# Output projection of a hybrid encoder block by one level of Strassen's scheme

## The chip, the cores and the metric

The kernel runs on one core of a Trainium2 chip. The metric is the device time of one execution in microseconds (us), of which the median of several runs is compared. Below, "the projection" is the product of the gated sum m with W_o, and "the MLP's first layer" is what follows it.

## What is computed

The kernel computes one block of an encoder on 1024 tokens of width 1024 (MLP width 4096). The part that the change touches is the line with `w_o`:

```python
merged = jax.nn.sigmoid(ga) * y_a + jax.nn.sigmoid(gb) * y_b
x = x + merged @ w_o[l]
h = rms_norm(x, norm2_g[l]) @ w_mlp_in[l]
x = x + jnp.square(jax.nn.relu(h)) @ w_mlp_out[l]
```

All operands are float32. A matmul of the kernel works on float16, so each operand is scaled by a power of two and split in a high half (float16 of the value, made by ACT) and a low half (float16 of the remainder, made by DVE), and each product is run in three passes (high by high, high by low, low by high, `PASSES`). A product of 1024x1024 by 1024x512 in plain form is thus 8 token blocks x 8 channel blocks x 3 passes = 192 matmuls of 128x512.

## The kernel before, in words

**Order of the work.** After attention and the convolution, eight gate stages n = 0 to 7 run, one for each 128 channels of m. A stage computes both gates of its channels by a Strassen level already (`seven`, L1273: 7 products of 12 matmuls, 18.1 us) and the two branch products (`branch_units`, L1331: 48 matmuls). Stages 0 to 6 do the gates first. Stage 7 does the branches first (503.97 to 514.33 us in the trace) and its gates last (514.33 to 532.48), with a sigmoid and a product for each half of the tokens (`post7`, `post3`, `last`). Each m_n is split by `m_done` (`last` for n = 7) into mH and mL, [128, 8 channel blocks, 1024 tokens].

**The projection** (532.48 to 615.60) comes next: columns 0 to 511 of W_o are the chunk cO[0], columns 512 to 1023 are cO[1]. A call of `proj(b, half)` (L1605) is a unit of 24 matmuls of 128x512 for token block b, and its result is added to the residual X1 by one DVE instruction (L1610). There are 16 such units. Their weights are split by `Chunk.prep` (L280: ACT L343, DVE L330), with a maximum of each row (L362) and a sum over all partitions by a small matmul (`all_sum`, L226) behind one cast (L372), from which the scale follows.

**The MLP's first layer** then takes two strips of 256 columns in two halves each (`quad`, 615.60 to 633.90 and 633.90 to 652.30: 14 units of 12 matmuls of 128x256) and 14 strips of 512. It needs the normalised rows of X1 in Strassen forms: blocks b and b+4 are a pair, and for each pair n the ACT squares the rows (`square`, L1430), DVE and ACT make the factor (`row_scale`, L1436), ACT applies it (`normal`, L1442), DVE makes four sums and differences (`form_sums`, L1480), ACT the highs and DVE the lows (`high`, `low`, L1468 and L1472). `first1`/`prep1(0)` makes the first strips' weights beside it (lines L1234, L1238; sums on POOL, L1221). The second layer follows to the end.

**What sets the order.** Each engine runs its own queue strictly in the order in which the program emits the instructions. `unit` (L233) emits a unit's matmuls, then the posts (the instructions that read the results) of the unit before, then it advances generators: `step` those of the list `fg`, `tick` those of the list `bg`, one piece at a time. A generator yields at `yield`, and `yield WAIT` gives the turn back. So where a piece of preparation stands in an engine's queue depends on how many units, steps and ticks came ahead of it. PSUM results rotate through eight banks named ps_d, ps_s and ps_o; a unit can start only when the post of the unit that last used its bank is done. Weights come by DMA into five raw buffers; a new load starts when `done` counts a finished one (`load_upto`).

## Time and profile before

| | |
|---|---|
| median of 3 runs (lowest to highest) | 1201.63 us (1200.84 to 1201.65) |
| profiled execution, its own time | 1201.78 us |
| span from the first to the last instruction | 1200.0 us |
| granted TensorE clock | 1.00 |
| gate products of stage 7 | 514.33 to 532.48 |
| projection | 532.48 to 615.60 (384 matmuls of 128x512) |
| first two half strips of the MLP | 615.60 to 633.90, 633.90 to 652.30 |

The execution's own time and its span differ by 1.8 us, which lie outside the instructions. PE is TensorE with its matmuls, PEld its weight loads, DVE, ACT and POOL are the vector, scalar and GpSimd engines. The profile gives the busy time of each; `a <-b` behind a row's idle time says that the engine stood idle before it and that b ended that. The table of windows gives a stretch's length, then the busy time (and number of instructions) of PE, PEld, DVE, ACT and POOL in it, then the granted clock, the DMA share and GB/s.

### The profile page before, as it was taken

How to read it: one execution, taken by the hardware profiler on the slowest of the kernel's cores; microseconds unless marked ns; L12 is line 12 of the kernel's file. 1: busy time of each engine (PE TensorE's matmuls, PEld its weight loads, DVE VectorE, ACT ScalarE, POOL GpSimd, SP SyncE). 2: the span in 40 equal slices, each digit the busy share in tenths (PEclk: the TensorE clock that was granted, in tenths of full speed). 3: DMA queues.
4: the chain of work that ended last, by engine and by line, in shares of the span. 5: the costliest groups of instructions: out<-in, count | busy, mean ns of one | idle time of the engine just before them, and what ended most of it. 6: DMA issues, size and time to landing. Idle time of an engine off the chain costs nothing.

```text
span 1200.0 us, 16982 instructions
## 1 busy us (share of the span) xinstructions
PE 1190.2 (99%) x6272; PEld 574.7 (48%) x6272; DVE 940.3 (78%) x1750; ACT 752.1 (63%) x1181; POOL 450.9 (38%) x296
## 2 busy tenths in 40 slices
...
GB/s 259 201 153 126 107 96 145 124 163 117 135 121 58 54 70 36 71 116 165 60 170 195 174 142 192 160 130 193 153 242 220 356 73 193 158 120 214 105 36 105
DMA packets 162707, 171.25 MB, mean 143 GB/s; under 512 B 123328, under 2 KB 123840, under 8 KB 158528
## 3 DMA queue, kind: packets, MB, share of 16 engines
...
## 4 chain that ended last, share of the span: by engine, by line
PE 84%; DVE 11%; ACT 2%; issue 1%; DMA 1%; SPq 0%; ACTq 0%
PE ps_d L236 27%; PE ps_s L236 24%; PE ps_o L236 20%; PE ps_d L1067 5%; PE ps_d L669 2%; PE ps_d L718 2%; PE ps_s L718 2%; DVE P L95 2%; PE ps_s L669 2%; DVE w_s L1234 1%; DVE sz L95 1%; DVE sc L95 1%; DVE w_ws L95 1%; DVE sg L1357 1%; DMA xt<-in_x 1%
## 5 line engine op out<-in xcount | busy, mean ns | idle before, releaser
L236 PEld LDWEIGHTS <-ops 128*128 128x128 f16 x1356 | 132.5, 98 | 157.3
L236 PEld LDWEIGHTS <-w 128*128 128x128 f16 x1368 | 132.8, 98 | 139.4
L1067 PE MATMUL ps_d<-uT,w_ws 128*128 128x512 f16 x576 | 128.0, 379 | 0.3 <-DVE cv L95 0.3
L236 PE MATMUL ps_s<-ops 128*128 128x512 f16 (+1 forms) x504 | 114.3, 376 | 0.0
L236 PE MATMUL ps_d<-ops 128*128 128x512 f16 x492 | 112.9, 379 | 0.0
L236 PE MATMUL ps_d<-u2T,w 128*128 128x512 f16 (+1 forms) x504 | 110.1, 371 | 0.0
L1847 ACT ACTIVATE ops<-hf,sc 128x2048 f16<-128x2048 f32 x26 | 52.0, 1998 | 84.8 <-PE ps_d L236 47.2
L1221 POOL TENSOR_TENSOR tsum<-raw 128x512 f32<-128x512 f32 x28 | 48.2, 1737 | 139.3 <-DVE v L1475 74.2
L1425 POOL TENSOR_TENSOR as<-as 128x512 f32<-128x512 f32 x60 | 82.9, 1382 | 41.6 <-ACT as L1707 38.1
L236 PEld LDWEIGHTS <-w_s 128*128 128x128 f16 x588 | 56.8, 98 | 69.0 <-DVE w_s L1234 1.2
L1067 PEld LDWEIGHTS <-w_ws 128*128 128x128 f16 x576 | 54.6, 98 | 65.6 <-issue 1.5
L236 PE MATMUL ps_o<-ops 128*128 128x512 f16 (+1 forms) x360 | 81.3, 375 | 0.0
L236 PE MATMUL ps_s<-u2x,w 128*128 128x512 f16 (+1 forms) x348 | 78.6, 375 | 0.0
L1849 DVE SCALAR_TENSOR_TENSOR ops<-hf,sc,ops 128x2048 f16<-128x2048 f32 x26 | 74.8, 2876 | 3.2 <-ACT ops L1847 2.2
L1099 ACT ACTIVATE raw<-raw,sc 128x256 f32<-128x256 f32 x164 | 67.5, 494 | 1.9 <-DMA raw<-in_weights 1.9
L1221 POOL TENSOR_TENSOR gsum<-raw 128x512 f32<-128x512 f32 x14 | 19.3, 1394 | 127.8 <-issue 53.6
L1238 ACT ACTIVATE w<-raw,sc 128x512 f16<-128x512 f32 (+1 forms) x28 | 24.6, 927 | 50.8 <-DVE sc L475 50.8
L1740 DVE TENSOR_TENSOR as<-ps_s,as 128x512 f32<-128x512 f32 x13 | 9.0, 692 | 57.9 <-ACT as L1759 57.9
L1321 ACT ACTIVATE sg<-sg,sc 128x2048 f32<-128x2048 f32 (+1 forms) x7 | 13.2, 1880 | 52.2 <-DVE sg L1319 52.2
L1863 POOL TENSOR_TENSOR raw<-raw 128x1024 f32<-128x1024 f32 x8 | 30.8, 3870 | 36.5 <-DVE ops L1857 36.5
L236 PE MATMUL ps_o<-u2T,w 128*128 128x512 f16 (+1 forms) x204 | 44.2, 366 | 0.0
L236 PEld LDWEIGHTS <-mH 128*128 128x128 f16 x304 | 29.6, 98 | 30.4
...
## 6 DMA issues: line engine op xcount, KB each, us to landing
...
xt<-in_x SPq DMA_DIRECT2D x8, 512.0 KB, 10.2
...
x<-in_x SPq DMA_DIRECT2D x8, 512.0 KB, 10.6
```

Of the source, the lines that this page charges most:

```text
L95: return f(out, *a, **kw)
L236: T.matmul(ps, l, r, start=a, stop=b)
L669: T.matmul(ps, UT[:, sa, k, b * 128:(b + 1) * 128], w, start=(kind, k) == ("hh", 0), stop=(kind, k) == ("hl", 7))
L718: T.matmul(vbank["q", b], UT[:, sa, k, b * 128:(b + 1) * 128], cQ.parts[:, sw, 512 * k:512 * k + 512], start=(k, n) == (0, 0), stop=(k, n) ...
L1067: T.matmul(ps, l, r, start=a, stop=b)
L1099: A.activation(v, v, AF.Copy, scale=sc[:, at(g, 4 * i + k)])
L1221: G.tensor_tensor(t[:, o], a, b, op=OP.add)
L1238: A.activation(o(0), w, AF.Copy, scale=sc[:, s])
L1425: sub.tensor_tensor(z[o], z[a], z[b], op=op)
L1847: A.activation(P[:, 1, 0], hf, AF.Copy, scale=sc[:, Rs])
L1849: V.scalar_tensor_tensor(P[:, 1, 1], hf, sc[:, Rs], P[:, 1, 0], op0=OP.mult, op1=OP.subtract)
L1863: G.tensor_tensor(w11[i2], w11[i2], w12[i2], op=OP.add)
```

## The change

**Products.** The projection uses one Strassen level in each half h of the columns. The rows' halves are the token blocks (b, b+4), the columns' halves are the 256-column parts of the half, and the contraction's halves are the even and the odd channel blocks, so a pair i = (2i, 2i+1) of m's channel blocks is what one form needs. Seven products of 4 pairs x 3 passes x 4 token blocks = 48 matmuls of 128x256 take the place of 192 of 128x512: 672 of 128x256 in all instead of 384 of 128x512.

**m.** m is kept by pairs (`mp`), and its 7 forms are made pair by pair (`m_forms`, 4 sums on POOL, highs on ACT, lows on DVE) during stages 2, 4 and 6. Pair 3 is formed during stage 7's gates, in `turned` and `last`, and the order of stage 7's products changes to 1, 2, 4, 5, 6, 7, 3.

**W_o.** `prep_o(h)` takes the place of `Chunk.prep` for cO[h]. For each of four quarters (128 channels x 2, [128, 4 parts, 256]) it makes highs and lows of forms 0 to 2, four sums in place on POOL (L1396 of the changed kernel, 128x256 each), then highs and lows of forms 3 to 6. In the loop over n the forms 3 to 6 of quarter n-1 are emitted ahead of forms 0 to 2 of quarter n.

**Results.** Half 0 runs in 14 units of 24 matmuls (two token blocks), order 1, 7, 6, 5, 4, 2, 3; half 1 in 28 units of 12 matmuls (one token block), order 1, 6, 7, 5, 2, 4, 3 for each. `o_post` combines them: product 1 is copied by ACT, the others go through DVE (L1767 of the changed kernel), with sums into X1 on POOL (L1770). Between the halves everything waits until `prep_o(1)` is emitted; the MLP's first weights (`first1`) wait in the program until half 0 is emitted (`o_half`).

Core of the diff:

```diff
+    def m_forms(i, m):
...
+        for o, a, b, op in ((3, 1, 3, OP.subtract), (1, 0, 1, OP.subtract), (0, 3, 0, OP.subtract), (2, 2, 0, OP.add)):
+            G.tensor_tensor(q[:, o], q[:, a], q[:, b], op=op)
...
+    def prep_o(h):
...
+        while not o_ready[0]:
+            yield WAIT
+        mul(rm, at(rowsM, 0, 4), rm)
+        V.tensor_reduce(sc[:, a], sc[:, rm], axis=AX, op=OP.max)
+        c, mark = ones_col(), units[0]
+        V.tensor_copy(c, sc[:, a])
+        yield
+        yield from apart(mark, 1)
+        yield from all_sum(c, b, anybank(), 1e-30)
...
+        for n in range(5):
+            r = [ch.raw[p].rearrange("p (f c) -> p f c", f=4) if 0 <= p < 4 else None for p in (n, n - 1)]
+            if n:
+                part(n - 1, 3, 7, r[1], 0)
+            if n < 4:
+                part(n, 0, 1, r[0][:, 0:1], 0)
+                part(n, 1, 3, r[0][:, 2:4], 0)
+            yield
+            if n < 4:
+                part(n, 0, 1, r[0][:, 0:1], 1)
+                part(n, 1, 3, r[0][:, 2:4], 1)
+                for o, x_, y_ in ((0, 0, 1), (1, 1, 3), (3, 0, 3), (2, 3, 2)):
+                    G.tensor_tensor(r[0][:, o], r[0][:, x_], r[0][:, y_], op=OP.add)
+            yield
+            if n:
+                part(n - 1, 3, 7, r[1], 1)
+                done[0] += 1
+                load_upto(done[0] + 5)
+                yield
...
             def last(sg, half):
                 o = slice(2 * half, 2 * half + 2)
                 V.tensor_tensor(sg[:, o], sg[:, o], y[:, o], op=OP.mult)
-                V.tensor_tensor(m[:, half], sg[:, 2 * half], sg[:, 2 * half + 1], op=OP.add)
-                t = slice(512 * half, 512 * half + 512)
-                A.activation(M[0][:, 7, t], m[:, half], AF.Copy, scale=sc[:, s7])
-                V.scalar_tensor_tensor(M[1][:, 7, t], m[:, half], sc[:, s7], M[0][:, 7, t],
-                                       op0=OP.mult, op1=OP.subtract)
+                d = 3 if half else 2
+                V.tensor_tensor(q[:, d], sg[:, 2 * half], sg[:, 2 * half + 1], op=OP.add)
+                m_high(3, d - 1 if half else 1, d if half else 2, row(d), s7)
...
-    push(cO[1])
-
-    def proj(b, half, acts=None, mms=None):
-        ps = anybank()
-
-        def fin():
-            o = X1[:, b, 512 * half:512 * half + 512]
-            V.scalar_tensor_tensor(o, ps, sc[:, cO[half].inv], o, op0=OP.mult, op1=OP.add)
...
+    PRODUCT = {1: (0, 0), 6: (4, 6), 2: (1, 1), 7: (5, 4), 5: (2, 3), 4: (3, 5), 3: (6, 2)}
...
+        if o == 1:
+            A.activation(a1, ps, AF.Copy, scale=inv)
+            put(x(0, 0), a1, OP.add)
+        elif o == 6:
+            into(a6, a1)
+            put(x(0, 1), a6, OP.subtract)
+        elif o == 7:
+            into(a7, a6)
+            put(x(1, 1), a7, OP.subtract)
+            put(x(1, 0), a7, OP.add)
+        elif o == 5:
+            into(x(1, 1)), into(x(0, 1))
         else:
+            into(x(*{2: (0, 0), 4: (1, 0), 3: (0, 1)}[o]))
...
+    bg.extend([prep_o(1), first1(), prep_m()])
...
+    for o in (1, 7, 6, 5, 4, 2, 3):
+        for j in (0, 2):
...
+            unit(o_mms(two[0], 0, o, j) + o_mms(two[1], 0, o, j + 1), post, 0, 6)
+    settle()
+    o_half[0] = 1
+    forced[0] = True
+    while w_ready[0] < 2:
+        tick()
+    forced[0] = False
...
+    tail(1, 1, sq(0), g1)
+    tail(1, 6, do(begin, 0), g1)
+    tail(1, 7, form_sums, g1)
...
+    tail(2, 6, do(begin, 1))
...
+    tail(3, 6, do(begin, 2))
```

**Where instructions stand now.** Three places follow. The first is ACT's queue at the end of stage 7's gates. Before, the last split of cO[0] (tile w_ws) stood there as one run, ahead of the two sigmoids (L1315, L1321) and the two highs of m (L1391):

```order
L1325 ACTIVATE sg<-ps_o 128x512
L343 ACTIVATE w_ws<-raw,sc 128x512 x8
L1315 ACTIVATE sg<-sg,sc 128x1024
L1391 ACTIVATE mH<-m,sc 128x512
L1321 ACTIVATE sg<-sg,sc 128x1024
L1391 ACTIVATE mH<-m,sc 128x512
```

Of the change, the same queue from the first row of W_o's forms (tile w_o) on: 128x256 and 128x2x256 are forms 0 to 2 of a quarter, 128x4x256 the forms 3 to 6 of the quarter before it; u2T holds the forms of m's last pair, L1423 and L1429 are the sigmoids:

```order
L1382 ACTIVATE w_o<-raw,sc 128x4x256
L1382 ACTIVATE w_o<-raw,sc 128x256
L1382 ACTIVATE w_o<-raw,sc 128x2x256
L1423 ACTIVATE sg<-sg,sc 128x1024
L1307 ACTIVATE u2T<-m,sc 128x512 x3
L1382 ACTIVATE w_o<-raw,sc 128x4x256
L1382 ACTIVATE w_o<-raw,sc 128x256
L1382 ACTIVATE w_o<-raw,sc 128x2x256
L1382 ACTIVATE w_o<-raw,sc 128x4x256
L1429 ACTIVATE sg<-sg,sc 128x1024
```

The first sigmoid and three highs of m now stand between the third quarter's forms 0 to 2 and its forms 3 to 6, and a quarter's forms 3 to 6 stand ahead of the next quarter's form 0.

The second place is DVE's queue over the same time. Before, the cast for half 1's scale (L372) stood behind the last low of m (L1392), four maxima over half 1's weights and the first post of the projection:

```order
L1392 SCALAR_TENSOR_TENSOR mL<-m,sc,mH 128x512
L362 TENSOR_REDUCE sc<-raw 128x2 x4
L1610 SCALAR_TENSOR_TENSOR x_5394<-ps_o,sc,x_5394 128x512
L150 TENSOR_TENSOR sc<-sc 128x8
L370 TENSOR_REDUCE sc<-sc 128x1
L372 CAST ones<-sc 128x1
```

Of the change, first from the last of the four sums of stage 7's product 7 (L1421; L1418 to L1420 stand ahead of it) to the lows of W_o's last two quarters:

```order
L1421 TENSOR_TENSOR sg<-ps_s,sg 128x512
L1527 TENSOR_TENSOR sg<-sg,gsum 128x1024
L1529 TENSOR_TENSOR m<-sg 128x512
L1532 TENSOR_TENSOR m<-m 128x512
L1534 TENSOR_TENSOR m<-m 128x512
L1313 SCALAR_TENSOR_TENSOR u2T<-m,sc,u2T 128x512 x3
L1380 SCALAR_TENSOR_TENSOR w_o<-raw,sc,w_o 128x256
L1380 SCALAR_TENSOR_TENSOR w_o<-raw,sc,w_o 128x2x256
L1380 SCALAR_TENSOR_TENSOR w_o<-raw,sc,w_o 128x4x256 x2
```

and right behind it, to the cast that the all-partition sum for half 1's scale waits for (L1364):

```order
L1427 TENSOR_TENSOR sg<-ps_s,sg 128x512
L1527 TENSOR_TENSOR sg<-sg,gsum 128x1024
L1529 TENSOR_TENSOR m<-sg 128x512
L1540 TENSOR_TENSOR m<-m 128x512
L1313 SCALAR_TENSOR_TENSOR u2T<-m,sc,u2T 128x512 x2
L1357 TENSOR_REDUCE sc<-raw 128x1 x4
L150 TENSOR_TENSOR sc<-sc 128x4
L1362 TENSOR_REDUCE sc<-sc 128x1
L1364 CAST ones<-sc 128x1
```

The low of the fourth quarter's form 0 now stands behind the first half's sigmoid (ACT L1423, which L1527 needs), its product and the lows of m; the cast stands behind the fourth quarter's forms, the second half's sigmoid (ACT L1429) and the four maxima.

The third place is PE's queue: where the small matmuls of the all-partition sums (L227) stand in the projection. Before, both stood together, after 96 matmuls of the projection:

```order
L236 MATMUL ps_o<-w_ws,mL 128x512
L227 LDWEIGHTS ones
L227 MATMUL ps_d<-ones 128x1
L227 LDWEIGHTS ones
L227 MATMUL ps_s<-ones 128x1
L236 LDWEIGHTS mH
```

Now one stands after the first 48 matmuls, that is, after product 1 (upper part), and the other, for the MLP's first weights, after product 5's first unit, the seventh of 14 (lower part):

```order
L236 MATMUL ps_d<-w_o,u2T 128x256
L227 LDWEIGHTS ones
L227 MATMUL ps_s<-ones 128x1
L236 LDWEIGHTS mK
L236 MATMUL ps_o<-w_o,mK 128x256
```

```order
L236 MATMUL ps_s<-w_o,u2T 128x256
L227 LDWEIGHTS ones
L227 MATMUL ps_o<-ones 128x1
L236 LDWEIGHTS mK
L236 MATMUL ps_d<-w_o,mK 128x256
```

The second of these waits for a cast (L1080) that stands in DVE's queue behind all lows of half 1's four quarters (L1380) and two posts of half 0 (L1767), as the piece from there shows (w_s and w_p are half 1's forms):

```order
L1380 SCALAR_TENSOR_TENSOR w_p<-raw,sc,w_p 128x256
L1380 SCALAR_TENSOR_TENSOR w_p<-raw,sc,w_p 128x2x256
L1380 SCALAR_TENSOR_TENSOR w_p<-raw,sc,w_p 128x4x256 x2
L1767 SCALAR_TENSOR_TENSOR as<-ps_s,sc,as 128x512
L1767 SCALAR_TENSOR_TENSOR as<-ps_o,sc,as 128x512
L1079 TENSOR_REDUCE sc<-sc 128x1
L1080 CAST ones<-sc 128x1
```

278 lines of the change are left out of this document (204 added, 74 removed).

## Prediction, written before the changed kernel was run

> **What bounds the kernel now.** I read the busy times first, then the chain that ended last by engine, then PE's waits.
>
> ```profile
> PE 1190.2 (99%) x6272; PEld 574.7 (48%) x6272; DVE 940.3 (78%) x1750; ACT 752.1 (63%) x1181; POOL 450.9 (38%) x296
> PE 84%; DVE 11%; ACT 2%; issue 1%; DMA 1%; SPq 0%; ACTq 0%
> PE ps_o L598 <- POOL u L585: 2.3, 1, 2.3
> ```
>
> PE is busy for 99% of the span, 84% of the last chain is PE, and its longest wait is 2.3 us, at the start. So PE sets the time as long as the others keep ahead. How far ahead they are where the change is, the table of windows says: stage 6, stage 7's gates, the projection, and the two half strips behind it.
>
> ```profile
> 482.00:503.00 21.00, 21.00 (x100) 9.55 (x99) 16.44 (x44) 9.21 (x13) 0.00 (x0) 1.00 0.18 52
> 514.33:532.48 18.15, 18.15 (x86) 8.24 (x85) 13.43 (x32) 7.80 (x12) 0.00 (x0) 1.00 0.16 49
> 532.48:615.60 83.12, 83.12 (x390) 37.79 (x389) 66.11 (x118) 55.14 (x85) 5.08 (x4) 1.00 0.53 145
> 615.60:633.90 18.30, 18.30 (x170) 16.40 (x169) 13.88 (x31) 14.65 (x25) 6.37 (x4) 1.00 1.01 161
> 633.90:652.30 18.40, 18.40 (x171) 16.45 (x169) 16.30 (x37) 15.70 (x25) 5.35 (x4) 1.00 0.47 151
> ```
>
> DVE has 17.0 us to spare in the projection's 83.1 and 4.4 in the half strip. The change takes time from PE and gives DVE, ACT and POOL more, so the question is whether PE still finds its operands ready.
>
> **PE's own price.** From the chain:
>
> ```profile
> 610.42 5.18 PE ps_s L236 x24
> 615.60 1.31 PE ps_o L236 x12
> ```
>
> A 512-wide matmul takes 5.18/24 = 0.2158 us, a 256-wide one 1.31/12 = 0.1092. So 384 x 0.2158 = 82.9 becomes 672 x 0.1092 = 73.4: **-9.5 us**. Weight loads stay hidden (PEld 16.40 of 18.30 in a stretch of 256-wide ones). That alone would give 1201.8 - 9.5 = 1192.3.
>
> **Pairs 0 to 2 of m** cost nothing in my sum: in stage 6 DVE has 4.6 us free, ACT 11.8, POOL all, and nobody needs these forms before the projection. If that cover is too thin, stages 2, 4 and 6 slip by up to about 1 us each: 0 to 3.
>
> **W_o's forms: one quarter's cycle.** ACT's queue has forms 3 to 6 of a quarter ahead of form 0 of the next, and these wait for the four POOL sums of that quarter, which wait for its lows of form 0 on DVE. So quarters run one after the other: ACT 128x4x256, ACT 128x256, DVE 128x256, four sums. The nearest rows:
>
> ```profile
> L1238 ACT ACTIVATE w_s<-gsum,sc 128x1024 f16<-128x1024 f32 x14 | 15.2, 1134 | 0.0
> L343 ACT ACTIVATE w_wa<-raw,sc 128x256 f16<-128x256 f32 x16 | 6.8, 497 | 6.1 <-DVE sc L303 5.8 <-POOL bT L904 0.3
> L330 DVE SCALAR_TENSOR_TENSOR w_wb<-raw,sc,w_wb 128x256 f16<-128x256 f32 x16 | 6.7, 483 | 5.6 <-ACT w_wb L343 5.6
> L904 POOL TENSOR_TENSOR bT<-cv,bT 128x256 f16<-128x256 f32 x16 | 11.0, 719 | 9.4 <-ACT bT L95 9.4
> L1221 POOL TENSOR_TENSOR gsum<-gsum,raw 128x512 f32<-128x512 f32 x14 | 18.0, 1285 | 3.0 <-ACT gsum L1108 2.4
> L1234 DVE SCALAR_TENSOR_TENSOR w_s<-gsum,sc,w_s 128x1024 f16<-128x1024 f32 x14 | 17.3, 1277 | 0.0
> ```
>
> A POOL sum of 128x256 in f32 is not in the trace; half of L1221 bounds it below (0.64), L904 with the same elements gives 0.72, which I take. 1.13 + 0.50 + 0.48 + 4 x 0.72 + 0.26 (four changes of engine, some 0.06 each) = **5.25 us**. Whether DVE works undisturbed beside POOL, three rows show:
>
> ```profile
> 640.45 3.70 DVE L1425 TENSOR_TENSOR as<-as 128x256 f32<-128x256 f32 x4
> 640.51 2.90 POOL L1221 TENSOR_TENSOR tsum<-raw 128x512 f32<-128x512 f32 x2 [7.53 <-ACT raw L1099]
> 648.80 1.80 DVE L1425 TENSOR_TENSOR as<-as 128x256 f32<-128x256 f32 x4 [0.69 <-ACT as L1707]
> ```
>
> The same four instructions took 3.70 us beside POOL and 1.80 without: 1.9 lost. With a loss of that size the cycle is 7.15. Only part of DVE's lows meets the sums, so I take the middle, 6.2, and keep both ends.
>
> The Trainium skill, SBUF — State Buffer, section "Who interferes with whom", says that a DVE instruction with two SBUF inputs contends with a GpSimd instruction that reads SBUF, for whole instructions. The trace agrees (3.70 against 1.80); by it alone the sum would use 7.15 throughout and end at the 1292 of the fourth rival.
>
> **First stall: the last quarter's form 0.**
>
> ```profile
> 525.56 0.22 DVE L303 TENSOR_SCALAR sc<-sc 128x8 f32<-128x8 f32 x1
> 525.81 5.01 ACT L343 ACTIVATE w_ws<-raw,sc 128x512 f16<-128x512 f32 x8 [8.06 <-DVE sc L303]
> 531.88 0.69 DVE L1310 TENSOR_TENSOR sg<-ps_d,sg 128x512 f32<-128x512 f32 x1
> 534.65 1.15 ACT L1315 ACTIVATE sg<-sg,sc 128x1024 f32<-128x1024 f32 x1 [3.82 <-DVE sg L1313]
> 535.83 1.23 DVE L1388 TENSOR_TENSOR sg<-sg,gsum 128x1024 f32<-128x1024 f32 x1 [1.22 <-ACT sg L1315]
> 538.57 0.75 DVE L1392 SCALAR_TENSOR_TENSOR mL<-m,sc,mH 128x512 f16<-128x512 f32 x1 [0.79 <-ACT mH L1391]
> ```
>
> Before, W_o's highs began at 525.81. Now a high and a low of m (0.72, 0.75) stand ahead of the scale: 527.4. First quarter without a predecessor: 0.50 + 0.48 + 2.88 + 0.15, sums done 531.4. Second quarter's forms 3 to 6 come 1.13 + 5.25 later on ACT, 537.8; DVE then does the third quarter's lows and these: 541.1. What stands behind them on DVE is priced by these rows and by
>
> ```profile
> L1425 DVE TENSOR_TENSOR form<-form 128x512 f32<-128x512 f32 x16 | 11.0, 690 | 1.6 <-ACT form L1443 1.2
> ```
>
> Four sums (4 x 0.69), the sigmoid on ACT (1.15), L1527 (1.23), three sums of 0.69 and three lows (0.75), ACT's forms 3 to 6 and form 0, and that low make 10.6 where rows of ACT and DVE that need not wait for each other are counted once: 551.7. Contention adds 2.4 (4.4 at most): **554** (551.7 to 556). PE gets there 9 matmuls after 532.48, at 533.5: a wait of **20.5 us**.
>
> **Second stall: half 1's scale.** After the wait 39 matmuls finish product 1, at 558.2, and then PE's queue holds the all-partition sum. Its cast waits on DVE: fourth quarter's POOL sums (2.88 + 0.7 contention), forms 3 to 6 on ACT and DVE (1.13 + 1.28), 560.2; L1427 0.69, sigmoid 1.25, 1.23, 0.69, 0.69, part of ACT's high 0.3, two lows 1.5: 566.6; then four maxima, priced by
>
> ```profile
> 544.55 4.59 DVE L362 TENSOR_REDUCE sc<-raw 128x2 f32<-128x1024 f32 x4
> ```
>
> (with the gap 4.8) and 0.9 of small ones: **572.3** (569 to 575), a wait of 14.1.
>
> **Third stall: the sum for the MLP's first weights.** PE has 5 units of 24 x 0.1092 = 2.62 ahead, until 585.4. The cast it then needs stands behind all lows of half 1. POOL first does four sums of 1.28 and two of the same size from X1, until about 577.5; the first quarter's sums end at 581, three cycles of 6.2 make 599.7, forms 3 to 6 2.4, two posts
>
> ```profile
> L1610 DVE SCALAR_TENSOR_TENSOR x<-ps_s,sc,x 128x512 f32<-128x512 f32 x6 | 4.5, 746 | 0.0
> ```
>
> of 0.75: **603.3** (597.4 to 609.4), a wait of 17.9.
>
> **Half 1 and the first half strip: DVE.** From 603.3 PE needs 7 units, 18.3, to 621.6, and DVE, waiting for their posts, gains no lead. Then PE has 28 x 1.31 = 36.7 for half 1. DVE has, until the post that frees the half strip's first bank, 21 posts of 0.48 (10.2), the MLP's lows (0.75 + 3 x 1.28 = 4.6), `prep_m` (5 x 0.75 + 4 x 0.69 = 6.5), two pairs' form sums and lows (8 x 0.69 + 8.2), small ones 2.5: 37.5. The rows for posts, lows and waits:
>
> ```profile
> L1957 DVE SCALAR_TENSOR_TENSOR x<-ps_s,sc,x 128x256 f32<-128x256 f32 x1 | 0.5, 484 | 0.6 <-PE ps_s L236 0.6
> 640.12 0.42 DVE L1761 TENSOR_TENSOR as<-ps_o,as 128x256 f32<-128x256 f32 x1
> L1475 DVE TENSOR_TENSOR v<-form,v 128x2048 f16<-128x2048 f32 x2 | 4.6, 2284 | 0.0
> L1475 DVE TENSOR_TENSOR v<-form,v 128x1536 f16<-128x1536 f32 x3 | 5.3, 1752 | 1.9 <-ACT v L1470 1.9
> L1475 DVE TENSOR_TENSOR v<-form,v 128x1024 f16<-128x1024 f32 x2 | 2.4, 1218 | 0.0
> L1433 ACT ACTIVATE u2x<-x 128x1024 bf16<-128x1024 f32 x6 | 6.3, 1051 | 5.0 <-DVE sc L230 2.7 <-issue 1.7 <-ACT raw L1470 0.5
> L1443 ACT ACTIVATE form<-x,sc 128x1024 f32<-128x1024 f32 x8 | 8.8, 1140 | 3.3 <-DVE sc L464 3.3
> ```
>
> Each pair waits on DVE for ACT's squares (2 x 1.05), a root, and two normalised rows (2 x 1.14), some 5; both pairs and the first ACT copies make 13, since DVE's queue holds these waits ahead of posts. 37.5 + 13 + 2.5 contention = 53 from 622.3: the half strip starts at **675.3** (667.5 to 681.4), before 615.60. In it DVE has 31 of its own (pairs 2 and 3, 16 results of 0.42) and some 7 of such waits: 39.3 with contention against PE's 18.30. The second half strip starts at **714.6** (705.1 to 720.4) instead of 633.90. From there on queues are as before; PE has no slack there to win it back.
>
> Sum: -9.5 + 20.5 + 14.1 + 17.9 + 53 - 36.7 + 0.7 + 39.3 - 18.3 = +81.0; by the two start times +80.7 (71 to 86.5). 1201.8 + 80.7 = 1282.5. The median stands 0.15 below the profiled execution: **1282**.
>
> **Rivals.**
> - *PE sets the time.* If POOL's sums were so short that the last quarter is there by 533.5, and DVE kept up, only -9.5 stays: 1192.3, faster. It decides at a cycle of about 1.7 us (three of them and form 0 between 527.4 and 533.5); the rows give 5.25. 0.04.
> - *Only the first stall is real.* DVE and ACT would use PE's 20 us to run ahead, and the later casts come in time: 1192.3 + 20.5 = 1213. Against it: in that stall PE waits for DVE itself, which so builds no lead. 0.06.
> - *Throughput alone.* If the order within queues cost nothing, DVE's 66.11 + 13.88 + 16.30 = 96.3 up to 652.3 would rise by 8 for lows (16 rows of 0.75 become 14336/8192 of it), 12 for posts (16 x 0.75 become 14 x 0.75 and 28 x 0.48), 5 for pair 3's extra sums and lows, and by 0 to 15 for POOL (8 x 1.9): 121 to 136 against 119.8, so 1203 to 1218. Against it: the cycle is a chain of four engines, not DVE's sum. 0.05.
> - *DVE and POOL take turns throughout.* The cycle is 7.15, the third stall ends at its upper end, 609.4 (+6.1), and half 1 and the half strip lose 3.5 more: 1282 + 9.6 = 1292. The rows 640.45 and 640.51 are for it; against it, the lows read their first input beside ACT's f16 result and stand beside only a part of the sums. 0.20.
>
> **How the numbers follow.** My forecast has 0.64, the rivals 0.35, and 0.01 is left for a time within 0.2%, which is about what a measurement can tell from none (2.4 us) and which no case gives. From the ends of the terms come 1201.8 + 71 = 1273 and 1201.8 + 86.5 = 1288. The 20 us of waits inside half 1 and the half strip are my least sure term; let them vanish beside other work (-20) or grow by half (+10, with rounding 11), and the ends are **1253 and 1299**. The first three rivals lie outside. Faster 0.04, slower 0.95.
>
> **What would show it.** Right: PE waits of 14 to 21 us each for DVE L1380, L1364 and L1080; the quarters of W_o 5 to 7 us apart on ACT; the second half strip starting near 715, and from there to the end the same 566 us as before. Wrong: no wait over 5 us at L227, ACT's forms of a quarter overlapping POOL's sums, or posts of half 1 that never hold PE.

## The result, and the profile after

| | before | after |
|---|---|---|
| median of 4 runs each (lowest to highest), us | 1201.45 (1200.84 to 1201.65) | 1300.43 (1297.73 to 1301.12) |
| ratio, with its 95% interval | 1 | 1.0821 (1.0802 to 1.0839) |
| span of the profiled execution, us | 1200.0 | 1298.4 |
| mean granted clock | 1.00 | 0.971 |

The changed kernel is 99 us slower. The prediction had the sign and the three stalls of the projection, and was 18 us too low; the time lies just above its upper end of 1299. The page of the kernel after, its busy times and the chain that ended last by engine:

```profile
PE 1202.6 (93%) x6560; PEld 609.4 (47%) x6560; DVE 986.2 (76%) x1786; ACT 769.9 (59%) x1206; POOL 524.9 (40%) x365
PEclk9999999999999999967898999999999999999999
PE 69%; DVE 17%; ACT 5%; issue 3%; POOL 3%; DMA 2%; SPq 0%; POOLq 0%; ACTq 0%; DVEq 0%
```

PE went from 99% busy to 93%, and from 84% of the chain to 69%. The busy time of PE rose by 12 us, where its work should have become 9.5 us shorter: the row PEclk has slices with less than full speed. PE's waits, with the total, the number and the longest:

```profile
PE ps_o L227 <- DVE ones L1080: 18.7, 2, 18.1
PE ps_o L236 <- ACT w_o L1382: 18.3, 3, 11.9
PE ps_s L227 <- DVE sc L1079: 12.2, 1, 12.2
```

These are the three stalls that were forecast: for W_o's first half (the 18.3 of the second row: 0.8, 5.6 and 11.9 us ahead of its second, third and last quarter), for half 1's scale (12.2), and for the sum behind the MLP's first weights (18.1). In the third row the cast L1364 and the sum L1079 stand next to each other on DVE, and the view names the one that came last.

The windows of the kernel after: stage 7's gates, half 0, half 1, and the first half strip. Columns as before: length, busy time and number of instructions of PE, PEld, DVE, ACT, POOL, granted clock, DMA share, GB/s.

```profile
527.93:546.09 18.16, 18.16 (x87) 8.25 (x86) 14.41 (x28) 4.36 (x8) 4.88 (x5) 1.00 0.00 0
546.09:641.29 95.20, 46.03 (x339) 36.81 (x338) 55.59 (x74) 33.77 (x55) 42.69 (x40) 0.71 0.23 89
641.29:694.04 52.75, 42.60 (x340) 34.73 (x337) 37.07 (x64) 26.94 (x35) 11.80 (x12) 0.90 0.27 50
694.04:732.15 38.11, 21.82 (x171) 17.19 (x169) 25.60 (x55) 25.43 (x43) 9.09 (x8) 0.91 0.69 127
```

Two things are to be seen. In half 0 no engine is near its limit (PE 46.03 of 95.20, DVE 55.59): so the work of one engine alone does not set its length; what does, the experiments ask. And stage 7's gates begin at 527.93, before any of the projection, where the kernel before began them at 514.33. Those 13.6 us are most of what the prediction missed.

**Where the 13.6 us were lost.** Two slips of about 7.2 and 6.3 us, both at places where a stage's gates follow the branch products of a stage in which a pair of m is formed. Ahead of the first one this execution was 0.7 us earlier than that of before, from its first 15 us on, and a last 0.8 came behind the third pair, at a sum in stage 6. The first slip on PE, before and then after:

```profile
391.81 3.05 PE L236 MATMUL ps_d<-qD,w_s 128*128 128x512 f16 x12
394.69 2.75 PE L236 MATMUL ps_s<-uT,w_s 128*128 128x512 f16 x12
```

```profile
391.44 0.61 PE L236 MATMUL ps_o<-uT,w_s 128*128 128x512 f16 x2 [2.60 <-ACT w_s L1248]
392.23 2.33 PE L236 MATMUL ps_o<-uT,w_s 128*128 128x512 f16 x10 [0.18 <-DVE w_s L1244]
...
397.58 2.74 PE L236 MATMUL ps_d<-qD,w_s 128*128 128x512 f16 x6 [2.42 <-DVE w_s L1244]
```

After, PE waits 2.60, 0.18 and 2.42 for the gate weights w_s. Before, it does not wait in this view; but one group of twelve took 3.05 instead of 2.75, so PE already stood some 0.3 us for them. There was no lead at this place, and whatever comes late passes to PE one to one. The clock adds some 1.5 us to it: behind the last of these waits six matmuls took 2.74, as long as twelve in the second row of before. At the second place PE waits for nearly the same times, and the clock stayed at 1.00. The weights come late because their scale does. DVE before, and then after (L475 is one of the small instructions that make the scale, L330 makes the lows of the branch weights):

```profile
373.19 1.68 DVE L330 SCALAR_TENSOR_TENSOR w_wa<-raw,sc,w_wa 128x256 f16<-128x256 f32 x4
...
385.43 0.14 DVE L475 TENSOR_SCALAR sc<-sc 128x1 int32<-128x1 int32 x1
```

```profile
372.46 4.70 DVE L330 SCALAR_TENSOR_TENSOR u2x<-raw,sc,u2x 128x256 f16<-128x256 f32 x4
...
380.75 1.27 DVE L1313 SCALAR_TENSOR_TENSOR mK<-m,sc,mK 128x1024 f16<-128x1024 f32 x1
...
384.59 1.27 DVE L1313 SCALAR_TENSOR_TENSOR mK<-m,sc,mK 128x1024 f16<-128x1024 f32 x1
...
390.49 0.14 DVE L475 TENSOR_SCALAR sc<-sc 128x1 int32<-128x1 int32 x1
```

and what ran on POOL beside the first of these rows:

```profile
372.62 5.67 POOL L1337 TENSOR_TENSOR m<-m 128x512 f32<-128x512 f32 x4 [6.66 <-DVE mK L1313]
```

The scale is 5.06 us later (390.49 - 385.43). Of that, 3.02 is the four lows that took 4.70 instead of 1.68 while POOL made the four sums of m's pair, and 2.54 the two new lows of m ahead of the scale in DVE's queue; DVE had begun 0.7 earlier. The Trainium skill, SBUF — State Buffer, section "Who interferes with whom", says that DVE and GpSimd share one pair of ports and that it is an exclusive lock; the two rows 372.46 and 372.62 agree with it in that the lows lost 3.02 us beside the sums; that one instruction shuts out the other for its whole time, they do not show.

**The clock.** The chain of the kernel after behind the third stall (start, length, piece), and the windows in that stall and behind it:

```profile
620.29 5.14 PE ps_d L236 x24
625.43 2.92 PE ps_s L236 x24
```

```profile
610.00:620.00 10.00, 0.00 (x0) 0.00 (x0) 6.13 (x9) 5.31 (x10) 6.17 (x6) 0.50 0.00 0
620.29:624.29 4.00, 4.00 (x21) 2.86 (x19) 3.22 (x10) 0.00 (x0) 4.00 (x5) 0.50 0.00 0
```

The wait begins at 602.0; the granted clock is 1.00 until 605, falls to 0.50 within the next microsecond, and stays there for over 5 us behind the wait: 24 matmuls take 5.14 and the next 24 take 2.92, where the forecast has 2.62 for each. That is 2.8 us more. The Trainium skill, TensorE: Matmul & The Clock Gate, section "What's actually happening", says that the clock halves after an idle window of about 3.4 us and comes back after a busy one; these rows agree with it for the long wait. A wait of 2.03 us in the experiment with 150 more matmuls, below, was followed by 0.50 as well, and there the measurement decides.

### The profile page after: what moved, and what is told of

It reads as the page before. It is cut to its first block, busy times and chain, and to the rows that moved or that the text cites. A ratio compares the mean times of both kernels' runs of the same rounds, so it can differ in the third digit from the quotient of the medians.

```text
span 1298.4 us, 17714 instructions
## 1 busy us (share of the span) xinstructions
PE 1202.6 (93%) x6560; PEld 609.4 (47%) x6560; DVE 986.2 (76%) x1786; ACT 769.9 (59%) x1206; POOL 524.9 (40%) x365
## 4 chain that ended last, share of the span: by engine, by line
PE 69%; DVE 17%; ACT 5%; issue 3%; POOL 3%; DMA 2%; SPq 0%; POOLq 0%; ACTq 0%; DVEq 0%
PE ps_d L236 23%; PE ps_s L236 18%; PE ps_o L236 16%; PE ps_d L1067 5%; POOL raw L1396 2%; PE ps_d L669 2%; PE ps_d L718 2%; PE ps_s L718 2%; DVE u2x L330 1%; DVE P L95 1%; DVE w_s L1244 1%; PE ps_s L669 1%; DVE sz L95 1%; DVE sc L95 1%; DVE sg L1481 1%
## 5 line engine op out<-in xcount | busy, mean ns | idle before, releaser
L236 PE MATMUL ps_s<-ops 128*128 128x512 f16 (+1 forms) x528 | 119.7, 377 | 0.0
L236 PE MATMUL ps_d<-ops 128*128 128x512 f16 (+1 forms) x492 | 111.6, 377 | 0.0
L1574 POOL TENSOR_TENSOR as<-as 128x512 f32<-128x512 f32 x60 | 82.9, 1381 | 41.6 <-ACT as L1910 38.1
L236 PE MATMUL ps_d<-u2x,w 128*128 128x512 f16 (+1 forms) x360 | 81.3, 377 | 5.0 <-DMA u2x<-w_o 5.0
L236 PE MATMUL ps_o<-ops 128*128 128x512 f16 x336 | 77.1, 379 | 0.0
L236 PE MATMUL ps_o<-u2T,w 128*128 128x512 f16 (+1 forms) x324 | 71.7, 371 | 0.6 <-DVE u2T L1767 0.6
L236 PEld LDWEIGHTS <-u2x 128*128 128x128 f16 x480 | 47.6, 100 | 48.6 <-issue 2.0
L1231 POOL TENSOR_TENSOR gsum<-raw 128x512 f32<-128x512 f32 x14 | 19.5, 1407 | 114.6 <-ACT raw L1099 53.6
L1943 DVE TENSOR_TENSOR as<-ps_d,as 128x512 f32<-128x512 f32 (+1 forms) x14 | 9.4, 672 | 57.9 <-ACT as L1962 57.9
L236 PE MATMUL ps_s<-u2T,w 128*128 128x512 f16 (+1 forms) x252 | 53.4, 363 | 0.0
L1429 ACT ACTIVATE sg<-sg,sc 128x2048 f32<-128x2048 f32 (+1 forms) x7 | 13.2, 1880 | 63.5 <-DVE sg L1427 63.5
```

Of the source, the lines that this page charges most:

```text
L236: T.matmul(ps, l, r, start=a, stop=b)
L1231: G.tensor_tensor(t[:, o], a, b, op=OP.add)
L1574: sub.tensor_tensor(z[o], z[a], z[b], op=op)
```

## The experiments

In what follows, "sum 1" is PE's all-partition sum for half 1's scale (after: 585.81), "sum 2" the one behind the third stall (620.10), and "the stretch" is the time from half 1's first matmul (641.29) to the second all-partition sum from there (730.88, one unit ahead of the end of the first half strip; the expectations call it the sum in the second half strip): 89.6 us. Each kernel was timed against the kernel before in three rounds; ratios are to it. Moments in a kernel are those of its one profiled execution, and the executions differ by up to 1.8 us from their first microseconds on. Lines of a kernel with lines taken out are a few lower than those of the kernel after.

### What the pairs of m cost

The theory is that POOL's sums and DVE's new lows make the gates late; the rivals, that something else of the change does it (weights, loads, m's highs on ACT).

**No sums of m's pairs.**

```diff
-        for o, a, b, op in ((3, 1, 3, OP.subtract), (1, 0, 1, OP.subtract), (0, 3, 0, OP.subtract), (2, 2, 0, OP.add)):
-            G.tensor_tensor(q[:, o], q[:, a], q[:, b], op=op)
```

> Leaves out the four POOL sums of pairs 0 to 2 of m (their forms 3 to 6 are made from unsummed values). In the changed kernel stage 7's gates start at 527.93 us instead of 514.33. Theory A: the sums of a pair take DVE's time while they run (the lows of the branch weights took 4.70 us instead of 1.68), and two lows of 1.27 us stand in DVE's queue ahead of the scale for the next gate's weights, which had no slack; both pass on to PE one to one at the two places where gates follow branches (stages 2 to 3 and 4 to 5), and the idle PE then runs some us at half clock. Without the sums some 3.0 of 5.8 us go at each place: stage 7's gates start at 520 to 523, and the time falls by 5 to 8 us to about 1294. Theory B: only the lows' place in the queue counts, and the sums run where DVE would wait anyway: start at 527 to 528, time the same within 1 us. Theory C: new homes of the branch weights and of the last activation form (buffers that were two slots of a pool) cause the slip: start 527 to 528.

Measured: 1293.21 us (1291.90 to 1294.86), ratio 1.0772 (1.0754 to 1.0790). The gates of stage 7 begin at 521.97, 6.0 earlier. DVE of this kernel:

```profile
372.68 1.67 DVE L330 SCALAR_TENSOR_TENSOR u2x<-raw,sc,u2x 128x256 f16<-128x256 f32 x4
...
387.29 0.14 DVE L475 TENSOR_SCALAR sc<-sc 128x1 int32<-128x1 int32 x1
```

The lows are back at 1.67, and the scale is 3.2 us earlier: it was POOL beside DVE that stretched them.

**No sums, and the lows of forms 3 to 6 replaced by copies on ACT.**

```diff
         for a in (3, 5):
-            m_low(i, a, a + 2, q[:, a - 3:a - 1], s)
+            for c, d, t in PLACES[i]:
+                u, v = max(a, c), min(a + 2, d)
+                if u < v:
+                    A.activation(t[:, u - c:v - c, 1], q[:, u - 3:v - 3], AF.Copy, scale=sc[:, s])
```

> As the run without the sums of pairs 0 to 2, and the lows of their forms 3 to 6 are written by ACT as plain copies of the scaled values instead of by DVE (the same bytes are written). Theory A: DVE now has about what it had before, so no PE wait of more than 0.5 us ahead of stages 3 and 5, stage 7's gates start at 514 to 516, and the time falls by 12 to 14 us from the changed kernel's 1300, to about 1287, which is the forecast plus the terms that were off by clock. Theory B (place of the lows alone): the same start as A. Theory C (buffers): 527 to 528 and no change of time.

Measured: 1285.61 us (1285.18 to 1286.08), ratio 1.0704 (1.0688 to 1.0720); the gates of stage 7 begin at 514.88. The scale and PE's wait in this kernel:

```profile
385.53 0.14 DVE L475 TENSOR_SCALAR sc<-sc 128x1 int32<-128x1 int32 x1
```

```profile
392.63 2.33 PE L236 MATMUL ps_d<-qD,w_s 128*128 128x512 f16 x10 [0.59 <-DVE w_s L1244]
```

The scale is where it was before (385.43), and of the 13.6 us 13.05 are gone. So the sums on POOL and the lows of forms 3 to 6 on DVE are together nearly the whole loss. The rivals are refuted, since the weights, loads, buffers and m's highs of the change are all still there; ACT's additional copies cost nothing visible.

**m's forms at other places, nothing left out.** If only the place is wrong, moving the lows and sums between the branch weights' lows, and the last two lows into the gap in which DVE waits for the sigmoid, should give most of it back.

```diff
+        for _ in range(2):
+            yield
         m_low(i, 0, 1, q[:, 0:1], s)
-        yield
         m_low(i, 1, 3, q[:, 2:4], s)
...
+        for _ in range(3):
+            yield
         for a in (3, 5):
             m_low(i, a, a + 2, q[:, a - 3:a - 1], s)
-            yield
...
-            while forming[0] < n // 2:
-                step()
-
-            def post(g, half, ps, iv, sg=sg, m=m):
+            def post(g, half, ps, iv, sg=sg, m=m, n=n):
...
                 if g == 1:
+                    while forming[0] < n // 2:
+                        step()
```

> Computes the same as the changed kernel; in the making of the forms of m's pairs 0 to 2 the first lows and the POOL sums come after the first half of the branch weights' lows, and the last two lows stand in DVE's queue in the gap in which it waits for the sigmoid (2.07 us). Theory A (place in DVE's queue and DVE's loss beside POOL): the lows of the branch weights take 1.7 + 1.7 to 3 us instead of 4.7 + 1.7, and only some 0.5 us of the last two lows pass on, so 1 to 2.5 us of slip are left at each of the two places instead of 5.8 and of the half clock behind it less; stage 7's gates start at 516 to 521 instead of 527.9, and the time falls by 7 to 12 us. Theory B (the amount of work on DVE): start at 525 to 528, time the same within 2 us.

Measured: 1296.15 us (1294.08 to 1299.07), ratio 1.0792 (1.0775 to 1.0808); gates at 523.90, later than I expected. DVE and POOL of this kernel show why:

```profile
372.40 1.68 DVE L330 SCALAR_TENSOR_TENSOR u2x<-raw,sc,u2x 128x256 f16<-128x256 f32 x4
...
378.20 4.24 DVE L330 SCALAR_TENSOR_TENSOR u2x<-raw,sc,u2x 128x256 f16<-128x256 f32 x4 [0.58 <-ACT u2x L343]
...
390.19 0.14 DVE L475 TENSOR_SCALAR sc<-sc 128x1 int32<-128x1 int32 x1
```

```profile
376.33 5.43 POOL L1338 TENSOR_TENSOR m<-m 128x512 f32<-128x512 f32 x4 [10.11 <-DVE sc L160]
```

The first four lows are free again, and the sums now stand beside the second four, which take 4.24 instead of 1.68. The contention only moved. The scale came only 0.3 us earlier, but PE came 1.9 us later to this place (its last branch products began at 387.95 instead of 386.08): 1.1 us of that this execution was behind from its start, and the rest it waited at a sum just ahead. So PE's first wait for gate weights fell from 2.60 to 0.45:

```profile
391.15 0.60 PE L236 MATMUL ps_o<-uT,w_s 128*128 128x512 f16 x2 [0.45 <-ACT w_s L1248]
```

The same fall of 2.15 us stands at the second place. It is about the gap of 2.07 us in which DVE used to stand before the sigmoid's result, and which the lows now fill. At the first place the clock also stayed at full speed behind the waits, 1.5 us more. That the gates came 4.0 us earlier, close to 2 x 2.07, is thus in part chance: the gains are larger, and the late start and the waits at the sums take some of them back.

### What makes the stalls of half 0

The theory of the prediction is the cycle ACT, DVE, POOL, ACT of each quarter; the rivals are DVE's load and a common throughput limit.

**No sums in W_o's forms.**

```diff
-                for o, x_, y_ in ((0, 0, 1), (1, 1, 3), (3, 0, 3), (2, 3, 2)):
-                    G.tensor_tensor(r[0][:, o], r[0][:, x_], r[0][:, y_], op=OP.add)
```

> Leaves out the four POOL sums in each quarter of W_o's forms (forms 3 to 6 are made from unsummed weights); the order of ACT and DVE stays. Theory A (the cycle of four engines): without 4 x 0.8 us and the time that DVE loses beside them a quarter takes 2.5 to 3.5 us instead of 6.5. The first stall of 18.7 us falls under 9, half 1's forms take 32 - 14 = 18 us at most and the third stall falls under 5; the time falls by 22 to 32 us to 1268 to 1278. Theory B (DVE's and ACT's own work sets these stretches): a quarter stays above 5 us and the time falls by less than 8 us.

Measured: 1269.49 us (1267.96 to 1272.51), ratio 1.0569 (1.0552 to 1.0586), 30.9 us less than after. PE's waits in this kernel:

```profile
PE ps_o L236 <- ACT w_o L1382: 10.9, 1, 10.9
PE ps_s L227 <- DVE ones L1364: 8.1, 1, 8.1
...
PE ps_o L227 <- DVE ones L1080: 3.3, 2, 2.6
```

The three stalls go from 18.3, 12.2 and 18.1 to 10.9, 8.1 and 2.6. In the kernel after, the 32 sums keep POOL busy for 31.0 us, so nearly the whole of their own time was on the path, although POOL is busy for 40% of the span. Without the sums DVE's losses beside them are gone too; how much the order alone makes, the next run asks.

**Forms 0 to 2 and the sums of all quarters first, then forms 3 to 6.** The same work without the chain from quarter to quarter.

```diff
-        for n in range(5):
...
+        for n in range(4):
+            part(n, 0, 1, r[n][:, 0:1], 0)
+            part(n, 1, 3, r[n][:, 2:4], 0)
             yield
+            part(n, 0, 1, r[n][:, 0:1], 1)
+            part(n, 1, 3, r[n][:, 2:4], 1)
+            for o, x_, y_ in ((0, 0, 1), (1, 1, 3), (3, 0, 3), (2, 3, 2)):
+                G.tensor_tensor(r[n][:, o], r[n][:, x_], r[n][:, y_], op=OP.add)
+            yield
+        for n in range(4):
+            part(n, 3, 7, r[n], 0)
+            yield
+            part(n, 3, 7, r[n], 1)
```

> Computes the same; the loop that makes W_o's forms emits forms 0 to 2 and the POOL sums of all four quarters first, then forms 3 to 6 of all four. Theory A (the cycle): quarters are serial since forms 3 to 6 of one stand on ACT ahead of form 0 of the next, 6.5 us a quarter as measured. With the new order product 1's weights are ready some 5 us after the scale, so the first stall (18.7 us in all) shrinks to under 4, the POOL sums run back to back (16 x 0.8 = 13 us), the sum for half 1's scale comes 8 to 15 us earlier, and the third stall's chain is 31 us minus 8 to 12. Time falls by 18 to 30 us, to 1270 to 1282. Theory B (throughput of DVE beside POOL): what DVE and POOL have to do is the same, so the time falls by less than 6 us, and the waits only change their names.

Measured: 1290.79 us (1290.63 to 1292.30), ratio 1.0750 (1.0734 to 1.0766): 9.6 less than after, between the two theories. PE's waits, and a row each of ACT and POOL of this kernel:

```profile
PE ps_s L227 <- DVE sc L1079: 22.5, 1, 22.5
```

```profile
585.47 1.70 ACT L1099 ACTIVATE raw<-raw,sc 128x256 f32<-128x256 f32 x4 [7.98 <-DMA raw<-in_weights]
```

```profile
546.41 11.86 POOL L1392 TENSOR_TENSOR raw<-raw 128x256 f32<-128x256 f32 x12 [0.36 <-DVE w_o L1380]
```

The first stall is gone (2.1 us are left), and sum 1 came at 578.31 instead of 585.81, so the second stall grew from 12.2 to 22.5. From 541.6 to 578.3 DVE has almost no gap: lows, the gates' posts, lows and four maxima are its own work, and this is now the limit. The cycle was thus worth some 7.5 us here, and behind it DVE's own work is the limit. Half 1's forms took 24 us instead of 32, but they started late: ACT, which makes them, stood 7.98 us for a load of the MLP's weights that its queue had ahead of them. So sum 2 was at 611.62, 8.5 earlier.

**The same, with the MLP's weights taken up behind half 1's forms.**

```diff
-        while not ch.raw:
+        while not ch.raw or w_ready[0] < 2:
             yield WAIT
```

> Computes the same; the order of W_o's forms as in the run with forms 0 to 2 first, and the scaling of the MLP's second strip's weights moves behind half 1's forms on ACT. In the former run ACT stood idle for 7.98 us at that scaling, until its load had landed at 585.47, since the loads follow the finished quarters, which come later in that order. Theory A: with the scaling out of the way, half 1's forms start at 580 instead of 587.65, their chain of 24 us ends at 604, and the time falls by 5 to 8 us below that run's 1290.8, to 1283 to 1286. Theory B: the scaling is needed soon behind, and its load and its sum only move the wait: within 2 us of 1290.8.

Measured: 1285.55 us (1284.60 to 1286.78), ratio 1.0703 (1.0684 to 1.0722), 5.2 less than the kernel above, and sum 2 at 606.46, 5.2 earlier. The wait for the load was on the path, behind the cycle.

**The sum for half 1 emitted three units later.** If PE's place in the queue matters, and not DVE, PE could do more ahead of the sum.

```diff
-        yield from apart(mark, 1)
+        yield from apart(mark, 1 if h == 0 else 4)
```

> Computes the same; the all-partition sum for half 1's scale stands two units of 24 matmuls later in PE's queue, and by that the sum for the MLP's first weights is emitted ahead of half 1's forms, so that its cast no longer stands behind them on DVE. Theory A (each stall is PE's queue holding a sum too early): the waits of 12.2 and 18.1 us at the sums go; half 1's forms still take 32 us from their scale, now beside 10 units (26 us) of half 0 instead of 5 (13 us), so a wait of 4 to 10 us appears at half 1's first weights, and the time falls by 8 to 16 us. Theory B (one chain through W_o's forms and then DVE sets the end, and where PE waits for it is all one): the waits go to half 1's first unit in full and the time stays within 3 us.

Measured: 1296.60 us (1294.86 to 1296.90), ratio 1.0789 (1.0772 to 1.0806). PE's waits:

```profile
PE ps_d L227 <- DVE ones L1080: 19.3, 3, 18.2
...
PE ps_d L227 <- DVE x L1767: 7.8, 1, 7.8
```

The sum for half 1's scale now stands behind 120 matmuls instead of 48 and does not wait. The sum for the MLP's first weights, which stood behind 168, now stands ahead of it, behind 96, and waits 18.2; a sum inside half 1 waits 7.8 for a post (L1767). Half 1 begins 15.5 us earlier (625.76), but its stretch takes 101.1 us, 11.5 more. 3.8 us were won in the median: most of what PE did not wait in half 0 it waited in half 1.

**150 more matmuls during the third wait,** to see what the clock costs.

```diff
+            if o == 5 and j == 0:
+                for _ in range(150):
+                    T.matmul(two[0], m_at(0, 0, 0)[:, 0:128], WO[0][0][:, 0, 0, 0:256], start=True, stop=True)
```

> Computes the same; 150 extra matmuls of 128x256 on weights and activations that are there stand in PE's queue ahead of product 5's first unit, into the bank that this unit overwrites. They take 16.4 us of the 18.1 us that PE waits for the third sum. Theory A (clock): after that wait PE runs at half clock for some 3 us (24 matmuls took 5.14 us, then 2.92, instead of 2.62), the recorded clock is 0.5 there, and this lies on the path, since DVE waits for PE's results. With PE busy until shortly before, the clock stays at 1.0, half 0's rest takes 18.3 instead of 21.1 us, and the time falls by 2 to 4 us. Theory B: what follows is set by DVE and ACT, and the 2.8 us are taken up by a shorter wait in half 1: time within 1 us of the changed kernel's. Both: the wait of 18.1 at the third sum becomes 1 to 3 us, and the sum itself comes at the same moment.

Measured: 1298.43 us (1297.91 to 1300.03), ratio 1.0809 (1.0792 to 1.0826), which overlaps that of after. The chain of this kernel behind the third sum:

```profile
619.52 4.31 PE ps_d L236 x24
623.83 2.62 PE ps_s L236 x24
```

PE stood 2.0 us instead of 18.1, and 48 matmuls took 6.93 instead of 8.06. The trace shows 1.1 us less. The granted clock was 1.00 all through the 150 matmuls and the wait, then fell behind it, and was 0.50 from 621.0 to 622.9. That the last 2 us of waiting made it fall is likely, but no run without them was made. By the times alone the experiment decides nothing.

### What makes half 1 and the half strips long

The stretch was 89.3 to 89.7 us in the kernel after and in seven of the eight kernels above (101.1 in the one with the sum emitted later, where half 1 began 15.5 us sooner), so it does not depend on when it starts, as long as it does not start far ahead of what it needs. The clock may be part of it: PE is busy for 63.2 us in it, where the same matmuls take 54 at full speed, and the granted clock is 0.90 on average; how much of these 9 us is on the path was not tried. A piece of it, in the chain that ended last of the kernel after:

```profile
669.69 2.21 DVE w_o L1623
672.03 6.90 DMA u2T<-w_o
679.03 0.47 ACT u2T L1773
```

The post L1773 copies a result of half 1 to a temporary that lies in a corner of the buffer u2T; a transpose into another part of u2T ends only at 678.9, and the copy stands behind it. Two things can be wrong here: the place of the temporary, and the order on DVE, where the lows L1623 stand ahead of posts:

```profile
669.62 2.27 DVE L1623 TENSOR_TENSOR w_o<-form,w_o 128x2048 f16<-128x2048 f32 x1
671.82 0.47 DVE L1767 SCALAR_TENSOR_TENSOR x<-ps_d,sc,x 128x256 f32<-128x256 f32 x1
672.21 1.74 DVE L1623 TENSOR_TENSOR w_o<-form,w_o 128x1536 f16<-128x1536 f32 x1
```

**The temporary in a buffer for weights, which is kept longer.**

```diff
-        held[0], limit[0] = 3, c1[2].first + 1
+        held[0], limit[0] = 4, c1[2].first + 1
...
-        held[0], limit[0] = 1, c1[3].first
+        held[0], limit[0] = 2, c1[3].first
...
-    one = u2T[:, 3, 1, :, 384:512].bitcast(F32)
+    one = rawp.tile([128, 1024], F32, name="raw")[:, 0:256].rearrange("p (a b) -> p a b", a=4)
```

> Computes the same; the temporary of half 1's posts lies in a raw weight buffer of its own instead of in a corner of the tile that the transposes of the MLP's activation forms write (one weight load of the third strip comes later for it). Theory A: half 1 is set by DVE's instructions and their waits for ACT, as forecast (53 us until the half strip); the time changes by less than 2 us. Theory B: half 1 is set by a chain through that tile. The trace shows ACT's post of the next token block wait for the transposing DMAs of the pair before (2.3 us idle behind 6.9 us of DMA, and once more), and the root for the next pair stands behind that post on ACT. Then three of 28 token-block steps lose 2 to 5 us each, and the time falls by 5 to 12 us.

Measured: 1313.61 us (1311.31 to 1314.64), ratio 1.0935 (1.0918 to 1.0951), 13 slower than after. The stretch is 87.8, so 1.8 shorter; but the strips behind it have one buffer for weights less, and there PE waits 13.5 us at two all-partition sums for their casts (10.7 the longer). The experiment changed two things, and its time tells nothing about the place of the temporary. So again:

**The temporary there, and the buffer given back in time** (the first and the third hunk above, without the second).

> Computes the same; only the temporary of half 1's posts moves to a raw buffer of its own, which is given back in time, so that the loads of the later strips are as before. In the earlier run with this temporary the buffer was kept, PE waited 10.7 us in the strips, and the time rose by 13 us. Theory A (false wait on the transposes, small): stretch from half 1's first unit to the sum in the second half strip 87 to 88.5 us, time 1 to 3 us below the changed kernel's 1300. Theory B (the buffer is missing anyway): time above 1303.

Measured: 1298.41 us (1295.55 to 1299.19), ratio 1.0812 (1.0794 to 1.0830); the stretch is 86.9. The place of the temporary costs 2.7 us of the 89.6; the time alone is not clear of that of after, whose interval it overlaps.

**The temporary there, and the lows of two pairs behind the posts of the next block.**

```diff
-    tail(1, 2, do(high, 0, 1), do(low, 0, 0))
-    tail(1, 4, do(low, 0, 1))
+    tail(1, 2, do(high, 0, 1))
+    tail(1, 4, do(tick, 0))
     tail(1, 3, sq(5))
-    tail(2, 1, sq(1))
+    tail(2, 1, sq(1), do(low, 0, 0), do(low, 0, 1))
...
```

> Computes the same; in half 1 the lows of the activation forms of pairs 0 and 1 (L1623 of the changed kernel) are emitted behind the posts and squares of the next token block instead of ahead of them, and the temporary of the posts lies in a raw buffer of its own that is given back in time. So far the stretch from half 1's first unit to the sum in the second half strip took 89.6 us in the changed kernel, 87.8 with the temporary elsewhere, 86.3 with the lows on ACT. Theory A (order on DVE): a pair's lows of 4 us stand between its sums and the posts that the next pair's squares wait for, on one chain through ACT and DVE of some 19 us a pair; behind the posts they run while ACT squares (2.5 us). For two of the pairs the chain is shorter by 2 to 3 us each, and by the 2 us of the temporary: the stretch takes 82 to 85 us and the time falls by 5 to 8 us. Theory B (transposing DMAs and the later need of the forms): the forms come later, and PE waits for them at the first half strip instead: stretch 86 to 90 us.

Measured: 1291.25 us (1290.62 to 1292.16), ratio 1.0751 (1.0735 to 1.0767); the stretch is 81.7. DVE of this kernel, at the same place of the program:

```profile
669.27 0.47 DVE L1767 SCALAR_TENSOR_TENSOR x<-ps_d,sc,x 128x256 f32<-128x256 f32 x1
...
670.44 3.95 DVE L1623 TENSOR_TENSOR w_o<-form,w_o 128x2048 f16<-128x2048 f32 x2
```

The posts come first, and no instruction was taken away: 5.2 us are the order on DVE alone (86.9 to 81.7).

**The lows of pairs 0 to 2 replaced by copies on ACT.**

```diff
-            V.tensor_tensor(v[:, :, 1], fv[0][:, a:b], v[:, :, 0], op=OP.subtract)
+            if n < 3:
+                A.activation(v[:, :, 1], fv[0][:, a:b], AF.Copy)
+            else:
+                V.tensor_tensor(v[:, :, 1], fv[0][:, a:b], v[:, :, 0], op=OP.subtract)
```

> The lows of the MLP's activation forms of pairs 0 to 2 are written by ACT as plain copies of the forms instead of by DVE as differences, at the same place of the program (L1623 of the changed kernel for these pairs, 2.2 + 1.75 us a pair on DVE). From half 1's first unit to the sum in the second half strip the changed kernel took 89.6 us, and 89.3 to 89.7 us in four of the runs so far, whatever came before. Theory A (as forecast): this stretch is set by DVE's queue, in which the posts of the next token block stand behind a pair's sums and lows; taking some 4 us a pair off it, of which ACT's copies give 1 back at most, shortens the stretch by 7 to 12 us, and the time falls by as much, to 1288 to 1294. Theory B: ACT's squares, root and normalised rows and the transposing DMAs set it, and DVE has room: the stretch keeps 88 to 90 us, or grows by what ACT has more (4 us a pair).

Measured: 1294.74 us (1294.38 to 1296.23), ratio 1.0781 (1.0763 to 1.0799); the stretch is 86.3. Taking the work from DVE altogether gave 3.3 us, less than leaving it there behind the posts. So DVE's busy time alone does not set the stretch; ACT, which got the copies here, is likely part of the chain as well (in the half strip it is busy for 25.43 us, as long as DVE). The most that any of these took from the stretch is 7.9 us (81.7, with the lows behind the posts). PE's own work in it at full speed is about 54 us (36.7 and 17), so most of the excess of about 36 us is still there in every kernel; it may lie in ACT's squares, highs and normalised rows, POOL's sums, the transposes and the clock, and how it is shared out among them stays open.

### Putting the mended parts together

**Forms first, weights later, and m's forms at their other places.** The edits of two kernels above.

> Computes the same; the changed kernel with the order of the run that makes forms 0 to 2 first and loads later (1285.6 us, 15 below the changed kernel) and with the forms of m's pairs 0 to 2 placed as in the run beside this one. Theory A: the slip of the gates and the stalls in the projection are separate terms of one sum, so the two gains add: 1285.6 less what that run gains, 1274 to 1279. Theory B: with the gates earlier, DVE's chain to half 1's scale is what ends last, and it starts with the gates; then the gains add as well for the slip, but if something outside (the loads of W_o's half 1 or of X1) sets the later sums, less than half of the second gain is left: above 1281. Either way it stays above the kernel before by some 75 us, of which half 1 and the half strip (89.4 against PE's 55) are 34.

Measured: 1282.92 us (1280.56 to 1283.95), ratio 1.0677 (1.0661 to 1.0693). Gates at 524.49. The second move gained 2.6 us here and 4.3 alone, so this is near Theory B's bound of 1281; but the stretch is 91.1 in this profile, 1.7 longer than in the one before, and the runs spread over 3.4 us, so the two theories are not told apart.

**The same with the lows behind the posts and the temporary moved.**

> Computes the same; all the moves that gained: forms 0 to 2 of W_o first with the scaling behind, forms of m's pairs placed in gaps, lows behind the posts, temporary elsewhere. Theory A: the terms add: 1282.9 less 5 to 8, 1275 to 1278. Theory B: what the later stretch gains is taken back by a load or a sum that is not ready: 1280 to 1284. Either way it stays 70 to 80 us above the kernel before.

Measured: 1273.31 us (1271.65 to 1274.63), ratio 1.0600 (1.0584 to 1.0616). The gains add up (27.1 us, where the three apart gave 14.9, 4.3 and 9.2, together 28.4). PE's waits in this kernel:

```profile
PE ps_s L227 <- DVE ones L1366: 22.0, 1, 22.0
PE ps_d L227 <- DVE ones L1080: 13.5, 3, 12.0
```

The time is a little below the range of Theory A. This is the fastest of the kernels that leave no work out, and it is still 72 us behind the kernel before. PE stands 34 us in two waits for casts on DVE (22.0 and 12.0), and the stretch is still 83.5.

## Why the prediction was wrong, point by point

| term | forecast, us | measured, us |
|---|---|---|
| stage 7's gates begin later by | 0 (up to 3) | 13.6 |
| from stage 7's gates to the end of the first stall | 39.7 | 38.9 |
| from stage 7's gates to sum 1 | 58.0 | 57.9 |
| from stage 7's gates to sum 2 | 89.0 | 92.2 |
| from sum 2 to half 1 | 18.3 | 21.2 |
| half 1 | 53.7 | 52.75 |
| first half strip | 39.3 | 38.1 |
| second half strip to the end | 566.1 | 566.25 |

Added to the forecast of 80.7, the 13.6 of the first row and the 4.0 that four later rows make together (to sum 2, from sum 2 to half 1, half 1 and the half strip: 3.2 + 2.9 - 0.95 - 1.2) give 98.3; the spans differ by 98.4.

**The step that failed** is "Pairs 0 to 2 of m cost nothing in my sum". It rested on a mean: in stage 6 DVE had 4.6 of 21 us free and POOL everything. But the free time does not lie where the pairs are formed. Where gates follow branches, the gate weights had no lead at all (the row of 3.05), and a stage's free time elsewhere is worth nothing to them. The price was wrong too: the rows 640.45 and 640.51 of the prediction, which show that DVE loses 1.9 us beside POOL, were applied to W_o's forms only. Applied to m's sums, which are of the same kind and larger, they give about 2 us for each pair, and with the new lows (2.5) 4.5 in place of "up to about 1", with no lead to swallow it; the forecast had at most 3 us for it. That the time still lies only just above the range is luck: its width was for waits in half 1, where the forecast was nearly right. The experiments without sums (lows back at 1.67), and without sums and lows (13.05 of 13.6 gone), show both parts.

**PE's own price** was right: 24 matmuls of 128x256 took 2.62 at full clock, 0.109 each. What was missing is the clock: the sum took full speed behind waits of 12 to 20 us. Where PE is the limit behind a wait, that cost 2.8 us (row "from sum 2 to half 1"); behind the first two stalls nothing hung on it, since PE still had to wait for DVE at the next sum.

**The quarter's cycle** was right in kind and nearly in size. Groups of sums on POOL in the kernel after, two of half 0 and the first of half 1:

```profile
547.93 4.32 POOL L1396 TENSOR_TENSOR raw<-raw 128x256 f32<-128x256 f32 x4 [2.18 <-DVE w_o L1380]
554.42 4.32 POOL L1396 TENSOR_TENSOR raw<-raw 128x256 f32<-128x256 f32 x4 [2.17 <-DVE w_o L1380]
...
592.07 3.12 POOL L1396 TENSOR_TENSOR raw<-raw 128x256 f32<-128x256 f32 x4
```

Two starts are 6.49 us apart; I had taken 6.2 between 5.25 and 7.15. The four sums took 4.32 and not 2.88, and the highs and lows with their changes of engine 2.17 instead of 2.37. The group at 592.07 met no DVE instruction and took 3.12, 0.78 for each sum; beside DVE's lows it is 1.08. The size that I took came from what DVE loses, and here POOL's own loss stands in the cycle.

**The three stalls** were right in place and order: 18.3 in all for W_o's first half (20.5 forecast), 12.2 for half 1's scale (14.1), 18.1 for sum 2 (17.9). The kernel without W_o's sums, which is 31 us faster, shows that these sums carry most of them; the one with the forms first shows that the order from quarter to quarter is only part of this, since there DVE's own work and POOL's sums, now back to back, are the next limits. Sum 2 came 3.2 us later than forecast: half 1's first sums ended at 595.2 (594.6 with the late gates counted in), three cycles took 19.5 instead of 18.7, and then DVE had to wait once more, which I had not seen:

```profile
619.70 0.15 DVE L1079 TENSOR_REDUCE sc<-sc 128x1 f32<-128x2 f32 x1 [1.08 <-ACT u2x L1692]
```

ACT squares rows of the MLP's weights (L1692) behind half 1's last forms, and the sum needs them. 0.6 + 0.8 + 1.1 are 2.5 of the 3.2; the rest are small instructions. The chain that ended last also passes through a load that the prediction does not have. POOL's first sum into X1 waited for the rows of x:

```profile
584.09 1.27 POOL L1770 TENSOR_TENSOR x<-x,as 128x512 f32<-128x512 f32 x1 [12.35 <-DMA x<-in_x]
```

Its other operand, ACT's copy of product 1, was there at 581.7, so the load held POOL for up to 2.4 us, and half 1's first sums of W_o stand behind it in POOL's queue. That they still began within a microsecond of the forecast is chance.

**Half 1 and the first half strip** came out within 1.2 us each, 52.75 for 53.7 and 38.1 for 39.3, but the reasons that I gave for them, DVE's load with its waits for ACT, are only partly shown, and the reduced clock in them was not forecast, so the good numbers are partly luck: of the some 36 us beyond PE's own work, the experiments take off 2.7 by moving the temporary, which the prediction did not see, and 5.2 by the order of lows and posts, which it did ("DVE's queue holds these waits ahead of posts"). The rest is open.

**The rivals.** "PE sets the time" and "throughput alone" are refuted by the windows: half 0 took 95.2 us with PE at 46.0 and DVE at 55.6. "Only the first stall is real" is refuted by the later waits of 12.2 and 18.1, and by the kernel with the forms first: without the first stall the second one grew to 22.5. "DVE and POOL take turns throughout" comes near for m's sums, where I had not looked (DVE lost 3.02 us beside 5.67 of POOL), and does not hold for W_o's, where the cycle was 6.49 and not 7.15. From the second half strip on the time was the same, 566.25 for 566.1.
